# The second half's keys, two blocks of filler matmuls, moved ahead of the first two pool projections in an RWKV-7 mixer

## The chip, the cores and the metric

The kernel runs on one core of a Trainium2 chip. The metric is the time of one execution on the device, in microseconds; runs are compared by their median. Engines are named as in the profile: PE is TensorE (PEld its weight loads), DVE is VectorE, ACT is ScalarE, POOL is GpSimd, SP is SyncE, which issues the loads of weights.

## What is computed

One block of a network on 256 tokens of width 2048, in fp32: a gated feed-forward part, a mixer, and a second gated feed-forward part, each with a norm ahead and behind and a residual. The mixer is what matters here:

```python
def _hybrid_mixer(u, w_in, ...):
    p = u @ w_in
    z_a, z_b, g_a, g_b = jnp.split(p, IN_SPLITS, axis=-1)
    y_a = _rwkv7_branch(z_a, ...) @ w_proj_a
    y_b = _pool_branch(z_b, pool_w, pool_scale) @ w_proj_b
    m = jax.nn.sigmoid(g_a) * y_a + jax.nn.sigmoid(g_b) * y_b
    return m @ w_out
```

`z_a` holds the keys, values and receptances (1024 columns each) of a recurrence over time with 16 heads, and some low-rank inputs. `z_b` goes through four moving averages over time and, per group of 256 columns, a product with `pool_w` (the mix). The two gates `g_a` and `g_b` have 2048 columns each.

## The kernel before

**Products.** Every matrix product is done in three matmuls on rounded parts: a weight tile of 128 x 1024 fp32 is loaded (L118), rounded by ScalarE (wH, L132), and VectorE takes the rest (wL, L133). The loaded tiles have 4 buffers, the parts 5 each. Two generators do the products of the mixer and hand out a cost after each step, so that they can be interleaved:

- `tok_g` (L254): 512 output columns, the tokens in two halves h, so two accumulator banks. A weight tile covers 2 k-steps, which is 12 matmuls (L156 to L158, three for each k and h). At the end an evacuation is called for each half.
- `ch_g` (L285): 256 output columns with the channels on the partitions, in one bank. A weight tile covers 4 k-steps, which is 24 matmuls (L298). At the end one evacuation.

Accumulator banks come from a ring of 4 (tag `mm`), temporaries of 128 x 512 from a ring of 4 (`tmp`, L83). A bank or a temporary is handed out again when its last use is over.

**Pieces of work.** Each is a generator in `mixer` (L537):

- `z_g(hf)` (L595): keys, values and receptances of half `hf` of the heads, in this order, two blocks of `ch_g` for each, with 16 k-steps. The evacuation is `shift` (L522): VectorE scales into a temporary (L527), ScalarE makes a shifted part in a shared buffer `zb` (L531), VectorE combines (L533).
- `gb_g(c)` (L617): a quarter of the second gate, `tok_g` with 16 k-steps. ScalarE evacuates with a sigmoid (L547), into two temporaries that live until the projection of the same quarter.
- `pb_g(c)` (L621): a quarter of the pool's projection, `tok_g` with 8 k-steps, on the scaled mixes `yb`. VectorE multiplies with the gate's temporaries (L625), and GpSimd stores the product to memory (L626). Quarter 0 has its gate from earlier, in a buffer of its own.
- `pool_mix` (L743): the product with `pool_w`; ScalarE scales the result into one part (L751), VectorE makes the other (L752).
- `p_g` (L629): the pool's windows and mixes; behind a `yield None`, the gate of quarter 1 with the last mix put in after 27 of its 32 steps.
- `rwkv` (L759): the recurrence of one half of the heads, a long dependent chain over all engines with few matmuls. It yields how much other work TensorE shall do before the next step.

**Order.** TensorE's order in this part is the order in which the matmuls are written, under a manual schedule. `weave` (L684) takes a step of the recurrence and then as much filler as this asks for. The filler is one sequence, `rest` (L668):

```python
def rest():
    yield from pg          # gate 1, last mix, end of gate 1
    yield from pb_g(0)
    yield from pb_g(1)
    yield from z_g(1)      # keys, values, receptances of half 1
    yield from gb_g(2)
```

and so on. The recurrence of half 0 takes filler up to the gate of quarter 2; that of half 1, which reads `z_g(1)`, follows. VectorE and ScalarE are not under the manual schedule here: their order is set by the framework's scheduler from priorities, which follow the order of emission, with a raised priority for the splits of weights and for the evacuations of `tok_g` and `ch_g`.

In what follows, pn, pV, pk, pA, pB, pb, pM, pX, pU, pSa, pS and pY are the names of the recurrence's results on TensorE in their order.

Of the kernel before, what the change touches and what calls it, by code (L numbers as in the profile page):

```python
# [52 lines left out]
class Block:  # L53
# [483 lines left out]
    def mixer(s, prm, uT, rs, resid, emit, gpost, reload):  # L537
# [54 lines left out]
        yT = [[s.unit((P, 4, S), F32R, n_) for n_ in ("yH", "yL")] for _ in range(2)]  # L592
        z = [{}, {}]

        def z_g(hf):  # L595
            for nme, zc in (("k", 1), ("v", 2), ("r", 0)):
                z[hf][nme] = s.unit((P, 4, S), F32, "z" + nme)
                for b in range(2):
                    c0 = zc * W + hf * 512 + b * 256

                    def ev_z(banks):
                        s.shift(banks[0], P, c0 // P,
                                [z[hf][nme][:, b * 2 + i] for i in range(2)])
                    yield from s.ch_g(w_in, c0, 256, at, NKD, ev_z, 8)
# [12 lines left out]
        def gb_g(c):  # L617
            sg = sgb[c] = [s.tmp("sgb"), s.tmp("sgb")]
            yield from s.tok_g(w_in, GB + c * 512, at, NKD, ev_sig(lambda h: sg[h]))

        def pb_g(c):  # L621
            sg = sgb[c]

            def ev_pb(h, ps):
                nc.vector.tensor_tensor(out=sg[h], in0=ps, in1=sg[h], op=ALU.mult)  # L625
                nc.gpsimd.dma_start(out=msp[c, :, h], in_=sg[h])  # L626
            yield from s.tok_g(prm["w_proj_b"], c * 512, at_b, NKW, ev_pb)
# [18 lines left out]
        def ga_g(c):  # L646
            sg = s.unit((P, 2, 512), F32, "sga")
            sga.append(sg)
            yield from s.tok_g(w_in, GA + c * 512, at, NKD, ev_sig(lambda h: sg[:, h]))
# [16 lines left out]
        pair = s.pair_g(prm["w_proj_a"], (0, 512), at_a, NKW, 4, (ev_pa(0), ev_pa(1)))  # L666

        def rest():  # L668
            yield from pg
            yield from pb_g(0)  # L670
            yield from pb_g(1)
            yield from z_g(1)
            yield from gb_g(2)
            yield from pb_g(2)
            yield from gb_g(3)
            yield from pb_g(3)
            for c in range(4):
                yield from ga_g(c)
            for t in pair:
                if t is None:  # L680
                    return
                yield t
# [8 lines left out]
        with s.tc.manual_schedule(engines={mybir.EngineType.PE}):  # L691
            for _ in s.ch_g(w_in, 3 * W, 288, at, NKD, ev_l, 4):
                pass
            pg = p_g()
            for g in (z_g(0), iter(pg.__next__, None)):
                for _ in g:
                    pass
            fill = rest()
            for hf in range(2):
                weave(chain(hf), fill)  # L700
            for _ in fill:
                pass
# [498 lines left out]
```

## Time and profile before

| | us |
|---|---|
| median of 3 runs | 2101.23 (2100.34 to 2101.69) |
| profiled execution | 2100.07 |
| its span | 2098.4 |
| TensorE busy | 2085.2 |
| VectorE busy | 1254.1 |
| ScalarE busy | 1111.3 |

The span goes from the first to the last instruction. Times in rows are microseconds from its start, unless marked ns; a name such as `sgb<-mm` is what an instruction writes and reads, without buffer numbers. Waits are inferred from semaphores: the engine named is the one that came last. A matmul's duration overlaps that of the next; the distance of their starts is what one costs.

### The profile page before, as it was taken

To read this page: it belongs to the slowest core of one execution; us is meant where nothing else is said; L and a number is where in the kernel's file an instruction comes from. 1 tells how busy PE (TensorE), PEld (TensorE's weight loads), DVE (VectorE), ACT (ScalarE), POOL (GpSimd) and SP (SyncE) were. 2 spreads that over 40 slices of the span, in tenths; PEclk is the share of its full clock that TensorE was granted. 3 is DMA by queue.
4 is the path that set the end of the run, shared out by engine and by line. 5 is a ranking of instruction groups with operands and counts; after the bars stand their busy time and mean duration, and the time that the engine had idled before them with its cause. 6 is when DMAs were issued, how large, how long until landed. Compare 5 with 4: busy or idle time off the path is not lost.

```text
span 2098.4 us, 28820 instructions
## 1 busy us (share of the span) xinstructions
PE 2085.2 (99%) x11089; PEld 1758.4 (84%) x11089; DVE 1254.1 (60%) x1588; ACT 1111.3 (53%) x1600; POOL 74.3 (4%) x161
## 2 busy tenths in 40 slices
PE   9999999999999999999999999999999999999998
PEld 7888888888888899989888788888888888888886
DVE  6555555555444565798688666575555555554444
ACT  6565555655444465464465444466655565554442
POOL 0000000000000010000110110000000000000000
PEclk9999999999999999999999999999999999999999
DMA  7656666577666666656456566666666666676664
GB/s 259 193 176 211 194 192 194 180 217 242 196 194 191 192 199 188 177 174 180 133 154 191 159 247 192 196 217 191 185 204 195 192 188 193 208 245 197 191 193 138
DMA packets 224116, 406.99 MB, mean 194 GB/s; under 512 B 13151, under 2 KB 49129, under 8 KB 223977
## 3 DMA queue, kind: packets, MB, share of 16 engines
q1 hardware_dynamic: 217801, 384.68, 60.0%
q0 software_dynamic: 5888, 19.93, 2.7%
q8 instruction: 87, 1.43, 0.3%
q10 hardware_dynamic: 288, 0.52, 0.1%
q14 instruction: 52, 0.43, 0.1%
HBM read 396.69 MB, written 8.39 MB: 193 GB/s over the span
## 4 chain that ended last, share of the span: by engine, by line
PE 97%; DVE 1%; issue 1%; ACT 0%; DMA 0%; DVEq 0%; POOLq 0%; POOL 0%; SPq 0%; ACTq 0%
PE mm L156 28%; PE mm L158 28%; PE mm L157 28%; PE mc L298 10%; PE tr L326 1%; PE pA L922 0%; DVE wL L133 0%; PE pSa L1030 0%; PE pU L1018 0%; DMA w<-in_ffn_gate_dram 0%; PE pT L1089 0%; PE pM L988 0%; PE pb L951 0%; PE pS L1038 0%; PE pY L1053 0%
## 5 line engine op out<-in xcount | busy, mean ns | idle before, releaser
L133 DVE TENSOR_TENSOR wL<-w,wH 128x1024 fp32r<-128x1024 f32 (+2 forms) x725 | 872.7, 1211 | 741.0 <-ACT wH L132 739.8
L132 ACT CAST wH<-w 128x1024 fp32r<-128x1024 f32 (+2 forms) x725 | 751.0, 1044 | 813.9 <-PE mm L158 665.9
L156 PE MATMUL mm<-wH,xH 128*128 128x512 f32 x2460 | 961.7, 392 | 0.0
L158 PE MATMUL mm<-wH,xL 128*128 128x512 f32 x2460 | 959.1, 390 | 0.7 <-DVE xL L334 0.7
L157 PE MATMUL mm<-wL,xH 128*128 128x512 f32 x2460 | 958.7, 390 | 0.0
L158 PEld LDWEIGHTS mm<-wH,xL 128*128 128x128 f32 x2460 | 461.9, 188 | 97.7 <-DVE xL L334 1.5
L156 PEld LDWEIGHTS mm<-wH,xH 128*128 128x128 f32 x2460 | 462.0, 188 | 96.0 <-ACT xH L332 0.4
L157 PEld LDWEIGHTS mm<-wL,xH 128*128 128x128 f32 x2460 | 462.1, 188 | 94.4 <-DVE wL L133 0.3
L298 PE MATMUL mc<-xH,wH 128*128 128x256 f32 x560 | 159.8, 285 | 0.0
L298 PE MATMUL mc<-xL,wH 128*128 128x256 f32 x560 | 158.7, 283 | 0.0
L298 PE MATMUL mc<-xH,wL 128*128 128x256 f32 x560 | 158.6, 283 | 0.0
L353 ACT COPY x<-T 32x256 f32<-32x256 f32 x352 | 141.8, 403 | 3.9
L298 PEld LDWEIGHTS mc<-xH,wH 128*128 128x128 f32 x560 | 106.1, 189 | 0.9
L298 PEld LDWEIGHTS mc<-xH,wL 128*128 128x128 f32 x560 | 106.1, 189 | 0.3
L298 PEld LDWEIGHTS mc<-xL,wH 128*128 128x128 f32 x560 | 106.1, 189 | 0.1
L372 ACT ACTIVATE sg<-mm,rs 128x512 f32<-128x512 f32 x44 | 29.9, 689 | 22.2 <-PE mm L158 22.2
L373 DVE SCALAR_TENSOR_TENSOR sg<-mm,rs,sg 128x512 f32<-128x512 f32 x44 | 31.5, 750 | 9.2 <-ACT sg L372 9.2
L405 POOL DMA_DIRECT2D gb<-in_ln_ffn_post_dram x4 | 2.4, 592 | 887.8 <-DVE xL L357 854.3
L360 ACT ACTIVATE junk<-mm 128x512 bf16<-128x512 f32 x24 | 14.4, 601 | 36.4 <-PE mm L158 36.4
L378 DVE SCALAR_TENSOR_TENSOR sg<-mm,rs,sg 128x512 f32<-128x512 f32 x44 | 30.9, 743 | 0.0
L343 DVE STREAM_TRANSPOSE T<-sg 128x512 f32<-128x512 f32 x44 | 30.8, 701 | 0.0
L156 PE MATMUL mm<-wH,yb 128*128 128x512 f32 x64 | 26.0, 407 | 1.8 <-ACT sgb L547 1.8
(245 smaller groups left out, 1071.1 us busy)
## 6 DMA issues: line engine op xcount, KB each, us to landing
w<-in_ffn_up_dram SPq DMA_DIRECT2D x176, 512.0 KB
w<-in_ffn_down_dram SPq DMA_DIRECT2D x176, 512.0 KB
w<-in_ffn_gate_dram SPq DMA_DIRECT2D x174, 512.0 KB
w<-in_w_in_dram SPq DMA_DIRECT2D x128, 512.0 KB
w<-in_w_out_dram SPq DMA_DIRECT2D x32, 512.0 KB
w<-in_w_proj_b_dram SPq DMA_DIRECT2D x16, 512.0 KB
w<-in_w_proj_a_dram SPq DMA_DIRECT2D x16, 512.0 KB
hsp<-fg POOLq DMA_DIRECT2D x16, 256.0 KB, 3.4
```

The lines of the kernel that those rows point to most:

```text
L132: s.nc.scalar.copy(vH, v)
L133: s.nc.vector.tensor_tensor(out=vL, in0=v, in1=vH.bitcast(F32), op=ALU.subtract)
L156: nc.tensor.matmul(ps, aH, bH, start=start, stop=False)
L157: nc.tensor.matmul(ps, aH, bL, start=False, stop=False)
L158: nc.tensor.matmul(ps, aL, bH, start=False, stop=stop)
L298: s.nc.tensor.matmul(o, lh, rh, start=one and n == 0, stop=k == KT - 1 and n == 2, skip_group_check=True)
L326: nc.tensor.transpose(ps[:, i], src[:, i * P:(i + 1) * P], s.ident)
L343: s.nc.vector.transpose(out=T1[:, h * 512:h * 512 + 512], in_=src)
L353: nc.scalar.copy(dst[q * 32:q * 32 + 32, :, :, i], src[i * 32:i * 32 + 32, :, :, q])
L372: nc.scalar.activation(out=sg, in_=ps, func=AF.Sigmoid, scale=rs[h])
L373: nc.vector.scalar_tensor_tensor(out=sg, in0=ps, scalar=rs[h], in1=sg, op0=ALU.mult, op1=ALU.mult)
L378: nc.vector.scalar_tensor_tensor(out=sig[h], in0=ps, scalar=rs[h], in1=sig[h], op0=ALU.mult, op1=ALU.mult)
```

## The change

The two blocks of keys of half 1 are taken out of `z_g(1)` and stand behind the pool's last mix (and the rest of gate 1) and ahead of the pool's first projection. Values and receptances stay where they were.

```diff
-        def z_g(hf):
-            for nme, zc in (("k", 1), ("v", 2), ("r", 0)):
+        def z_g(hf, part=0):
+            for nme, zc in ((("k", 1), ("v", 2), ("r", 0)), (("k", 1),),
+                            (("v", 2), ("r", 0)))[part]:
                 z[hf][nme] = s.unit((P, 4, S), F32, "z" + nme)
                 for b in range(2):
                     c0 = zc * W + hf * 512 + b * 256
...
         def rest():
+            z1 = z_g(1, 1), z_g(1, 2)
             yield from pg
+            yield from z1[0]
             yield from pb_g(0)
             yield from pb_g(1)
-            yield from z_g(1)
+            yield from z1[1]
             yield from gb_g(2)
```

## The prediction

> **What bounds the kernel now.** I read the page first, then TensorE's list of waits, the chain of waits around the longest of them, and the timelines of the engines there.
>
> ```profile
> span 2098.4 us, 28820 instructions
> PE 2085.2 (99%) x11089; PEld 1758.4 (84%) x11089; DVE 1254.1 (60%) x1588; ACT 1111.3 (53%) x1600; POOL 74.3 (4%) x161
> PE 97%; DVE 1%; issue 1%; ACT 0%; DMA 0%; DVEq 0%; POOLq 0%; POOL 0%; SPq 0%; ACTq 0%
> ...
> PE mm L156 <- ACT sgb L547: 1.8, 1, 1.8
> PE warm L223 <- POOL ident masks.py:199: 1.7, 1, 1.7
> PE mm L158 <- DVE xL L334: 0.7, 2, 0.5
> PE pSa L1030 <- ACT us L1025: 0.4, 1, 0.4
> PE tr L326 <- DMA x<-in_x_dram: 0.4, 1, 0.4
> ```
>
> The first three rows are the page's: TensorE is busy 2085.2 of 2098.4 us and is 97% of the chain. The other five are its complete list of waits (total, times, longest, in us). All of them together come to 5.0 us in 2098. So a change of order, which takes no instruction away, has little to win: at most these waits, and only one, the first, lies where the change is. The stretch looks like this on TensorE, and on the chain that ends there:
>
> ```profile
> 921.51 0.39 PE L156 MATMUL mm<-wH,yb 128*128 128x512 f32 x1
> 921.74 0.39 PE L157 MATMUL mm<-wL,yb 128*128 128x512 f32 x1
> 921.97 0.39 PE L158 MATMUL mm<-wH,yb 128*128 128x512 f32 x1
> 924.18 0.50 PE L156 MATMUL mm<-wH,yb 128*128 128x512 f32 x1 [1.82 <-ACT sgb L547]
> 924.52 0.40 PE L157 MATMUL mm<-wL,yb 128*128 128x512 f32 x1
> ```
> ```profile
> 921.15 0.48 DVE yb L752
> 921.65 0.47 ACT yb L751
> 922.14 1.28 ACT L547
> 923.44 0.70 ACT sgb L547
> 924.18 0.50 PE mm L156
> ```
>
> At 921.51 the first projection begins (its operand is yb). Three matmuls of its first half run; the first of its second half stands until 924.18. The columns of the second fence are start, duration, what. ScalarE first had the pool's last mix to scale (L751, itself behind VectorE's L752), then an activation table (1.28 us), then the first sigmoid of the gate (0.70 us). That sigmoid empties the bank which the projection's second half wants: of the four accumulator banks the gate took two, the mix the third, the projection's first half the fourth, and its second half comes round to the gate's first. The wait is thus one of the bank ring, one allocation too soon after the gate.
>
> Its price: from 921.97 to 924.18 is 2.21 us where the rows above it are 0.23 apart, so 1.98 lost, and the next step is 0.34 instead of 0.23, 0.11 more. **2.1 us.**
>
> **The change part by part.** TensorE's order is the written one. The two blocks of the second half's keys (z_g, part 1) move from behind the second projection to ahead of the first. Nothing is added or removed: the same loads, splits, matmuls, evacuations and stores.
>
> (a) The wait. A block of keys takes one bank, not two. The first block takes the bank that the first projection's first half has now, which had no wait at 921.51. The second block takes the gate's first bank, a block later.
>
> ```profile
> 963.15 43.91 PE mc L298 x366
> ```
>
> 366 of these matmuls in 43.91 us are 0.12 us each; a block is 16 k-steps of 2 column blocks of 3 matmuls, 96, hence 11.5 us. The gate's bank is asked for at 921.5 + 11.5 = 933.0 and is free at 924.1 by the chain above: 8.9 us to spare. The projections then take the mix's bank, the gate's second, and the two of the keys, each a block or more after its evacuation began. From the values on every bank is the same as before. So the 2.1 us go, and no bank is late next: **-2.1 us.**
>
> (b) The mix. The first projection reads the mix's last part.
>
> ```profile
> 928.09 0.48 DVE L752 SCALAR_TENSOR_TENSOR yb<-mc,cols,yb 128x256 fp32r<-128x256 f32 x1
> ```
>
> It is ready at 928.6, and read from the thirteenth matmul triple of the projection on, at about 931.8 now (924.18 and eleven triples of 0.68). That cover of 3 us becomes more than 20 us. It was no wait, so it is worth 0.
>
> (c) Weight tiles. With the wait gone, TensorE asks for its tiles 2.1 us earlier, while VectorE is nearly full:
>
> ```profile
> 918.00:938.00 20.00, 18.18 (x97) 14.66 (x97) 19.58 (x29) 10.99 (x15) 1.35 (x3) 1.00 0.63 196
> 938.00:958.00 20.00, 20.00 (x159) 17.29 (x156) 16.63 (x24) 14.99 (x32) 2.46 (x5) 1.00 0.70 226
> 958.00:978.00 20.00, 20.00 (x172) 19.59 (x171) 18.86 (x45) 8.31 (x12) 0.00 (x0) 1.00 0.56 153
> ...
> 924.25 1.22 DVE L133 TENSOR_TENSOR wL<-w,wH 128x1024 fp32r<-128x1024 f32 x1
> 929.34 0.39 PE L157 MATMUL mm<-wL,yb 128*128 128x512 f32 x1
> 929.89 1.23 DVE L133 TENSOR_TENSOR wL<-w,wH 128x1024 fp32r<-128x1024 f32 x1
> 934.78 0.39 PE L157 MATMUL mm<-wL,yb 128*128 128x512 f32 x1
> ```
>
> The table's columns after the length are the busy times of TensorE, its weight loads, VectorE, ScalarE and GpSimd, the granted clock, and the DMA share and rate: VectorE is busy 19.58 of 20 us. I counted the splits (L133) back from the steady stretch, where a cast waits for the end of the tile five before it. The split that starts at 924.25 is the third tile of the first projection and is used at 929.34; that of 929.89 is the first tile of the second projection, used at 934.78. They end at 925.47 and 931.12: leads of 3.9 and 3.7 us, or 1.8 and 1.6 us without the 2.1. A key tile lasts 24 x 0.12 = 2.88 us against 12 x 0.23 = 2.76 of a projection, so ahead of the third and the fifth tile, after two and four of them, the leads grow by 0.2 and 0.5, to 2.0 and 2.1 us. The splits hold, if VectorE keeps its order: **0**, with bounds of 0 and the price in rival C.
>
> (d) Evacuations and stores. Within the stretch up to the values they only change places:
>
> ```profile
> L527 DVE TENSOR_TENSOR z<-mc,rsb 128x512 f32<-128x512 f32 x6 | 4.1, 688 | 1.3 <-PE mc L298 1.3
> L531 ACT ACTIVATE zb<-z,cols 128x256 f32<-128x256 f32 x12 | 5.4, 501 | 0.2 <-DVE z L527 0.2
> L533 DVE SCALAR_TENSOR_TENSOR zk<-z,omu,zb 128x256 f32<-128x256 f32 x4 | 1.8, 481 | 0.0
> L625 DVE TENSOR_TENSOR sgb<-mm,sgb 128x512 f32<-128x512 f32 x4 | 2.7, 685 | 0.0
> L626 POOL DMA_DIRECT2D msp<-sgb x4 | 2.2, 559 | 19.0 <-DVE sgb L625 19.0
> ```
>
> A block of keys costs VectorE 0.69 + 2 x 0.48 = 1.65 us and ScalarE 2 x 0.50 = 1.0; a projection costs VectorE 2 x 0.685 = 1.37 and GpSimd two stores. So at about 933 and 946 VectorE has 0.3 us more than now and ScalarE 1.0 us more, and the long chain of small VectorE steps behind it (the recurrence's triangular inverse) has 0.3 us less per block. The recurrence's next step on TensorE is at 936.75:
>
> ```profile
> 931.03 1.38 DVE L898 TENSOR_TENSOR R<-R,R 64x512 f32<-64x512 f32 x2
> ...
> 936.75 1.99 PE pA L922 x32
> ```
>
> Its inputs are complete at 932.4 at the latest. TensorE will be there at 934.7, after the first block of keys (933.0), so 2.3 us lie between. I take 0. The lower bound is 0 as well, since TensorE does not wait there now; the upper is an evacuation of 1.65 us put wholly ahead of the inputs, which is less than the 2.3.
>
> (e) Temporaries. The gate's two tiles now live over the keys' two temporaries; with four buffers that just fits. The values' first evacuation takes the buffer that the second projection's first store frees.
>
> ```profile
> 988.38 0.69 DVE L527 TENSOR_TENSOR z<-mc,rsb 128x512 f32<-128x512 f32 x1 [0.27 <-PE mc L298]
> ...
> DMA to landing us min/median/max: 2.3/4.6/10.2
> ```
>
> The second projection will end where the keys' second block ends now, one block of 11.5 us and the 0.2 of the pipe ahead of that row, 976.7, less 2.1: 974.6. Two multiplications (1.4) and two issues (1.1) make 977.1; the median landing of a store gives 981.7, the worst one of the eight 987.3. The first evacuation of the values is now at 988.38, then at 986.3: 4.6 us to spare at the median, 1.0 us short at the worst, and behind that stand several split tiles. I take 0. [...]
>
> **The sum.** The profiled execution took 2100.07 us, its span 2098.4, so 1.7 lie around it. Less 2.1 it would be 2098.0, with a span of 2096.3. The median of the runs, 2101.23, is 1.16 above the profiled one; less 2.1 it is **2099.1 us**, 0.1% faster. The three runs spread from 2100.34 to 2101.69. About 0.2%, 4.2 us, is what a measurement of this kernel can tell from no change, so this counts as within it.
>
> **The rivals.**
>
> A (forecast), 0.72: the wait goes, nothing takes its place; 2099.1, with the spread of the runs 2098.0 to 2100.2.
>
> B, 0.15: the wait moves. TensorE runs 2.1 us earlier into engines that were not waiting for it, and meets a tile, an input of the recurrence or an evacuation that is late by as much. For it: VectorE at 19.58 of 20 us. Against it: the leads of 2.0 to 2.3 us in (c) and (d), and VectorE at 16.63 in the next stretch. 2101.2; and 2103.2 if a lead of 2 us is lost once more.
>
> C, 0.09, the other side: VectorE's order is not written here but follows from priorities, and a new order of emission can give a new one.
>
> ```profile
> L898 DVE TENSOR_TENSOR R<-R,R 64x512 f32<-64x512 f32 x4 | 2.7, 683 | 0.0
> L903 DVE SCALAR_TENSOR_TENSOR R<-R,R 64x504 f32<-64x504 f32 x4 | 2.7, 673 | 0.0
> ...
> 923.11 1.23 DVE L893 TENSOR_TENSOR R<-R,R 128x1024 f32<-128x1024 f32 x1
> ```
>
> If the recurrence's four L903, four L898 and the L893 between them (1.23 us) come ahead of the splits of the third to fifth tile, with the evacuation of a key block (1.65) and the mix's L752 (0.48), these are 8.8 us against a lead of 2.0: a wait of 6.8 us, 2099.1 + 6.8 = 2105.9. It costs from 2.0 us of delay on, and 0.2% above today's median, 2105.4, is reached at 8.3 us. Against it: the splits have a raised priority, and they do stand between those steps today.
>
> D, 0.04: a gain of more than 4.2 us. All waits of TensorE together are 5.0 us, 1.7 of them before any of this; I see no mechanism.
>
> That the change does not do what it says can hardly be: TensorE's order is fixed by the text.
>
> **How the numbers follow.** Faster by over 0.2%: D, 0.04. Slower by over 0.2%: most of C, 0.08. Within: the rest, 0.88. The range of 8 in 10 takes A and B: from 2097.5 (A, less the spread of the runs once more) to 2103.2 (B with a second lead lost).
>
> **What would show it.** Right: TensorE's list of waits without the row of sgb L547, and no new row above 0.5 us between 915 and 1035; the values begin at about 974.6 instead of 976.7, and everything behind is 2.1 us earlier; the span is 2096.3. Wrong: a wait of a matmul on a DVE wL between 925 and 940 (C), on z or zb between 933 and 950 (B), on a DVE z at 986 that itself waits for a store (e); or a sigmoid of the gate that still ends a wait.

## The result, and the profile after

| | before | after |
|---|---|---|
| median of 22 runs, us | 2101.72 (2099.93 to 2104.48) | 2098.38 (2097.79 to 2101.31) |
| profiled execution, us | 2100.07 | 2101.31 |
| its span, us | 2098.4 | 2099.6 |

The ratio of the runs is 0.9985, with a 95% interval of 0.9979 to 0.9991: 1.9 to 4.4 us faster, in the middle 3.2, or 0.15%. The forecast was 2099.1, that is 2.1 us faster, in a range of 2097.5 to 2103.2.

The profiled execution of the changed kernel is no typical one: it is the slowest of its 22, and its trace has to be read with that in mind. Its span of 2099.6 us is not the forecast 2096.3; the median span of the 22 runs is 2096.7. First its page and TensorE's complete list of waits (total, times, longest):

```profile
span 2099.6 us, 28824 instructions
PE 2087.3 (99%) x11089; PEld 1759.9 (84%) x11089; DVE 1253.8 (60%) x1588; ACT 1112.6 (53%) x1600; POOL 74.3 (4%) x161
...
PE warm L223 <- POOL ident masks.py:199: 1.7, 1, 1.7
PE tr L326 <- DMA x<-in_x_dram: 1.7, 1, 1.7
PE pSa L1033 <- ACT us L1028: 0.4, 1, 0.4
PE mm L158 <- DVE xL L334: 0.2, 1, 0.2
```

The row of `sgb L547`, 1.8 us, is gone, and no row has come in its place in the mixer. What made this execution long is at its very start. The table by stretches shows it (length; busy time of PE, PEld, DVE, ACT, POOL; granted clock; DMA share and rate):

```profile
0.00:10.00 10.00, 6.25 (x26) 4.66 (x26) 2.81 (x9) 4.64 (x12) 2.79 (x32) 0.92 0.76 268
10.00:20.00 10.00, 10.00 (x39) 7.88 (x39) 6.55 (x17) 5.03 (x12) 0.00 (x0) 0.74 1.05 385
20.00:30.00 10.00, 10.00 (x52) 8.23 (x51) 7.04 (x16) 6.57 (x17) 0.00 (x0) 1.00 0.51 188
...
890.00:1035.00 145.00, 145.00 (x1275) 133.58 (x1275) 125.53 (x238) 83.72 (x134) 14.95 (x24) 1.00 0.55 171
```

The matmul that waits for the input x starts at 7.30 us instead of 5.90 (a wait of 1.7 us against 0.4), and the granted clock was 0.92 and 0.74 in the first two stretches. In the changed stretch, the last row, TensorE is busy 145.00 of 145 us. In the profile of before it was 143.18:

```profile
890.00:1035.00 145.00, 143.18 (x1254) 131.02 (x1252) 124.47 (x236) 82.13 (x132) 14.96 (x24) 1.00 0.56 167
```

So that the start does not disturb the comparison, I set the two traces side by side: the start of TensorE's n-th matmul in one against that in the profile of before. Ahead of the change (matmul 4400, at 882 us) the changed kernel is 3.31 us late; behind it (matmul 5200, at 996 us) 1.21 us; at the last matmul 1.25 us. **The changed stretch gained 2.10 us, and nothing was lost or won behind it.** The same comparison is used for every run below.

| run | late at 882 us | late at 996 us | change in the stretch | late at the end |
|---|---|---|---|---|
| after | 3.31 | 1.21 | -2.10 | 1.25 |
| e1, before again | 0.39 | 0.36 | -0.03 | 0.38 |
| e2, first projection by halves | -0.05 | -2.14 | -2.09 | -2.11 |
| e3, keys between the projections | 0.38 | 0.27 | -0.11 | 0.30 |
| e4, gate without sigmoid | 0.90 | -0.56 | -1.46 | -0.52 |
| e5, one block of keys | 1.63 | -0.34 | -1.97 | -0.26 |
| e6, mix last | 0.24 | 3.17 | +2.93 | 3.20 |
| e7, 6.9 us more on VectorE | 0.00 | 9.15 | +9.15 | 9.21 |
| e8, longer gap | 0.37 | -1.74 | -2.11 | -1.07 |
| e9a, before, one more profile | 0.52 | 2.10 | +1.58 | 2.12 |
| e9b, before, one more profile | 0.44 | 0.45 | +0.01 | 0.48 |
| e9c, before, one more profile | 0.83 | 2.42 | +1.59 | 2.43 |
| e10, longer gap in one half | 0.16 | -1.95 | -2.11 | -1.33 |

Two questions were left. Are the 2.10 us the bank-ring wait alone (theory T), or does the keys' new place matter (rival K)? And why do the medians differ by 3.3 us when the traces differ by 2.1?

### The profile page after: what moved, and what is told of

The parts are those of the page before. It is cut to its first block, busy times and chain, and to the rows that moved or that the text cites. A ratio compares the mean times of both kernels' runs of the same rounds, so it can differ in the third digit from the quotient of the medians.

```text
span 2099.6 us, 28824 instructions
## 1 busy us (share of the span) xinstructions
PE 2087.3 (99%) x11089; PEld 1759.9 (84%) x11089; DVE 1253.8 (60%) x1588; ACT 1112.6 (53%) x1600; POOL 74.3 (4%) x161
## 4 chain that ended last, share of the span: by engine, by line
PE 98%; DVE 1%; issue 1%; DMA 0%; ACT 0%; DVEq 0%; POOLq 0%; POOL 0%; SPq 0%; ACTq 0%
PE mm L156 28%; PE mm L158 28%; PE mm L157 28%; PE mc L298 10%; PE tr L326 1%; PE pA L925 0%; DMA w<-in_ffn_gate_dram 0%; PE pSa L1033 0%; PE pU L1021 0%; PE pT L1092 0%; PE pM L991 0%; DVE wL L133 0%; PE pV L862 0%; PE pb L954 0%; PE pn L842 0%
## 5 line engine op out<-in xcount | busy, mean ns | idle before, releaser
L133 DVE TENSOR_TENSOR wL<-w,wH 128x1024 fp32r<-128x1024 f32 (+2 forms) x725 | 872.5, 1211 | 740.2 <-ACT wH L132 738.4
L357 DVE TENSOR_TENSOR xL<-x,xH 128x1024 fp32r<-128x1024 f32 x22 | 26.8, 1218 | 0.0
```

Source lines behind the costliest of these rows:

```text
L133: s.nc.vector.tensor_tensor(out=vL, in0=v, in1=vH.bitcast(F32), op=ALU.subtract)
L357: nc.vector.tensor_tensor(out=dL, in0=x32, in1=dH.bitcast(F32), op=ALU.subtract)
```

## The experiments

**e1: the kernel before, again.**

> The kernel before itself, once more, to see how much of the difference of 3.3 us between the medians lies in the changed stretch. Theory T (the bank-ring wait of 2.1 us is the whole effect of the change; the rest of the 3.3 us is chance at the start of the program, where the profile of the changed kernel lost 3.3 us before 90 us): its profile again has the wait of the first projection on the sigmoid of the gate, 1.8 us, and no other wait above 0.5 us between 890 and 1035; the runs spread by more than 2 us and spans go with the granted clock. Rival V (the wait is longer in other executions, which would make the gain more than 2.1 us): the wait in this profile is clearly longer or shorter than 1.8 us, say by 0.5 us or more.

Median 2100.39 us of 11 runs, ratio to the runs of before 0.9996 (0.9987 to 1.0005). The wait is again 1.8 us, so this profile gives no sign of a wait of another length (rival V); e9 adds three more profiles with the same 1.8 us.

**e2: the same wait taken away in another way**, with the keys left where they were (the kernel before; the diff is abridged, its comments are added, and only the first projection takes the new order).

```diff
-                for h in range(2):
-                    s.mm3(pss[h], ...)       # per k-step: half 0, half 1
+            for (k, wH, wL), h in [(t, h) for h in range(2) for t in ts]:
+                    s.mm3(pss[h], ...)       # per four k-steps: half 0, then half 1
```

> The order of before; only the first projection takes its steps differently: within each four k-steps first all of the first half of the tokens, then all of the second. The gate's bank is then asked for at 921.5 + 4 x 0.68 = 924.2 instead of 922.2, and it is free at 924.1. The keys stay behind the projections. Theory T: the wait falls from 1.8 us to under 0.3, the time by 1.8 to 2.1 us against before, the same as the change. Rival K (it is the keys' place that brings the gain: fewer evacuations beside the recurrence, a longer cover of the mix): the wait is gone but the time stays within 0.7 us of before, or another wait takes its place, such as a matmul on a split tile, for the second tile is asked for 1.4 us earlier.

Median 2098.40 us, ratio 0.9988 (0.9980 to 0.9997). TensorE's timeline, where the second half begins:

```profile
923.96 0.39 PE L158 MATMUL mm<-wH,yb 128*128 128x512 f32 x1
924.19 0.45 PE L156 MATMUL mm<-wH,yb 128*128 128x512 f32 x1
924.47 0.40 PE L157 MATMUL mm<-wL,yb 128*128 128x512 f32 x1
```

Four k-steps of one half are put between the gate's end and the claim on its bank, and the wait is gone: -2.09 us, as much as the change. The keys need not move for it. Theory T holds and rival K falls.

**e3: the keys between the two projections** (against the changed kernel).

```diff
             yield from pg
+            yield from pb_g(0)
             yield from z1[0]
-            yield from pb_g(0)
             yield from pb_g(1)
```

> The keys stand between the first projection and the second, not ahead of both. The first projection again follows the gate directly. Theory T: the wait on the gate's sigmoid is back, 1.8 us, and the time is that of before within 0.7 us. Rival K (an earlier place for the keys, apart from the banks, is what pays): half or more of the gain is kept, 1 us or more below before.

Median 2100.37 us, ratio 1.0000 (0.9991 to 1.0008). Its list of waits:

```profile
PE mm L156 <- ACT sgb L547: 1.8, 1, 1.8
PE warm L223 <- POOL ident masks.py:199: 1.7, 1, 1.7
PE pSa L1033 <- ACT us L1028: 0.4, 1, 0.4
PE tr L326 <- DMA x<-in_x_dram: 0.4, 1, 0.4
```

The keys stand earlier, but behind the first projection, and the wait is back at its full length.

**e4: no table at the gate.** The kernel before, with the sigmoid of the second quarter's gate left out; a scaled copy stands there. The diff is abridged.

```diff
-ev_sig(lambda h: sg[h])
+ev_sig(lambda h: sg[h], AF.Copy if c == 1 else AF.Sigmoid)
```

> The order of before; the gate of the second quarter leaves out its sigmoid (a scaled copy stands in its place), so that ScalarE loads no table there. Theory T, by the chain of before (the mix's scaling, table 1.28 us, sigmoid 0.70 us): the wait falls from 1.82 to about 0.5 us and the time by 1.3 us; the table is loaded at the next gate, near 1050, where nothing waits. Rival Y (the wait is set by the mix on VectorE and ScalarE, and the table is hidden): the wait stays above 1.3 us.

Median 2099.10 us, ratio 0.9992 (0.9983 to 1.0001). ScalarE's timeline and TensorE's one wait there:

```profile
922.55 0.47 ACT L752 ACTIVATE yb<-mc,cols 128x256 fp32r<-128x256 f32 x1 [0.56 <-DVE yb L753]
922.92 1.26 ACT L547 ACTIVATE sgb<-mm,rs 128x512 f32<-128x512 f32 x2
...
923.66 0.50 PE L156 MATMUL mm<-wH,yb 128*128 128x512 f32 x1 [0.41 <-ACT sgb L547]
```

Between the mix's scaling and the evacuation there is no table, and the wait is 0.41 us instead of 1.82. The table accounts for 1.4 us of the wait, the queue behind the mix for the rest. The interval of the medians holds 1, so it is the trace that shows this, with -1.46 us in the stretch.

**e5: only one of the two blocks moved** (against the kernel before, abridged).

```diff
-            yield from z_g(1)                      # behind pb_g(1)
+            yield from z_g(1, (("k", 1, 0),))      # ahead of pb_g(0)
+            ...
+            yield from z_g(1, (("k", 1, 1), ...))  # behind pb_g(1)
```

> Only the first of the two blocks of keys stands ahead of the projections; the second stays behind them. Theory T (the wait is one allocation of the four-bank ring too soon after the gate): one block in one bank is enough, since the first projection then comes round to the gate's banks 11.5 us later; the wait is gone and TensorE gains the whole 2.1 us in this stretch. Rival K (the gain grows with the work that is moved, through the evacuations and the cover of the mix): about half, 1.0 us.

Median 2098.36 us, ratio 0.9989 (0.9980 to 0.9998); -1.97 us in the stretch. One block does it all but 0.13 us; what these come from stays open. The gain does not grow with the work that is moved.

**e6: the mix behind the gate** (against the kernel before).

```diff
-            for t in itertools.islice(gate, 27):
-                yield t
-            yield from s.pool_mix(3, mix, prm["pool_w"], pT)
             yield from gate
+            yield from s.pool_mix(3, mix, prm["pool_w"], pT)
```

> The keys stay behind the projections; the last mix stands behind the whole gate instead of five steps ahead of its end. The gate ends 1.5 us sooner and its sigmoid is no longer queued on ScalarE behind the mix's scaling: table and sigmoid are done at about 922.0, when the projection's second half asks for the bank at 922.2. Theory T: the wait on the sigmoid falls to under 0.4 us. But the mix ends 3.4 us later and its last part, at 928.6 in before, is asked for at 929.7: if it comes 3.4 us later too, a wait of up to 2.3 us on VectorE or ScalarE making yb stands in its place. So between 2.1 us faster and the same as before; the change as made has no such price.

Median 2103.94 us, ratio 1.0014 (1.0005 to 1.0022): slower than before. TensorE's timeline, VectorE's up to the mix's row, and the stretches around it:

```profile
931.57 0.39 PE L157 MATMUL mm<-wL,yb 128*128 128x512 f32 x1
935.11 0.50 PE L158 MATMUL mm<-wH,yb 128*128 128x512 f32 x1 [3.15 <-DVE yb L750]
...
936.82 0.63 PE L158 MATMUL mm<-wH,yb 128*128 128x512 f32 x1
937.25 0.63 PE L156 MATMUL mm<-wH,yb 128*128 128x512 f32 x1
```
```profile
929.49 2.78 DVE L896 TENSOR_TENSOR R<-R,R 64x512 f32<-64x512 f32 x4
932.30 2.36 DVE L133 TENSOR_TENSOR wL<-w,wH 128x1024 fp32r<-128x1024 f32 x2
934.58 0.48 DVE L750 SCALAR_TENSOR_TENSOR yb<-mc,cols,yb 128x256 fp32r<-128x256 f32 x1
```
```profile
930.00:935.00 5.00, 1.96 (x9) 1.30 (x7) 4.93 (x8) 1.04 (x1) 0.00 (x0) 1.00 0.60 189
935.00:940.00 5.00, 4.89 (x15) 3.51 (x17) 3.61 (x5) 1.05 (x1) 1.15 (x2) 0.66 0.97 295
```

The wait on the sigmoid is gone as expected, and the other one stands in its place, with 3.15 us instead of "up to 2.3": the last part of yb is made at 934.58, six microseconds later than in before and not 3.4, for VectorE puts four steps of the recurrence (L896) and two splits ahead of it. But a gain of 2.1 and a wait of 3.2 make +1.1 us, and the trace shows +2.93. Most of the rest is in the last fence: behind the wait the granted clock falls to 0.66 in the mean of five microseconds, and the matmuls start 0.43 us apart (936.82, 937.25) instead of 0.23. That was the first sight of what the medians hid.

**e7: the load of rival C made to happen** (six more operations on VectorE, against the changed kernel).

```diff
+        for _ in range(0 if hf else 6):
+            V.tensor_tensor(out=fl(kk), in0=fl(kk), in1=fl(kk), op=ALU.max)
         V.tensor_tensor(out=fl(a), in0=fl(kk), in1=fl(a), op=ALU.mult)
```

> The changed kernel with six extra VectorE operations of 1.15 us each (6.9 us) in the recurrence of the first half, just ahead of L893; they leave its values as they are. It is the prediction's rival C made to happen: VectorE is given 6.9 us more in the full stretch where the splits lead by 1.9 to 2.1 us. If VectorE's order let the recurrence go ahead of the splits (rival C's mechanism), TensorE waits for split tiles, about 4.8 us in all. If the raised priority of the splits protects them, they keep at least 0.7 us of lead (one operation of 1.2 us put ahead of each) and it is the recurrence that is late: its first products, 4.7 us after their inputs now, wait about 2.2 us. Either way the stretch has room for 2 to 5 us of VectorE work, not for 7.

Median 2109.56 us of 5 runs, ratio 1.0041 (1.0028 to 1.0054). VectorE's timeline and TensorE's wait:

```profile
925.35 1.21 DVE L897 TENSOR_TENSOR R<-R 128x1024 f32<-128x1024 f32 x1
926.48 2.35 DVE L133 TENSOR_TENSOR wL<-w,wH 128x1024 fp32r<-128x1024 f32 x2
928.75 1.21 DVE L897 TENSOR_TENSOR R<-R 128x1024 f32<-128x1024 f32 x1
929.89 1.22 DVE L133 TENSOR_TENSOR wL<-w,wH 128x1024 fp32r<-128x1024 f32 x1
...
942.35 2.82 DVE L903 TENSOR_TENSOR R<-R,R 64x512 f32<-64x512 f32 x4
...
943.18 4.47 PE L927 MATMUL pA<-R,R 64*128 64x128 f32 x32 [8.55 <-DVE R L903]
```

The splits (L133) stand between the extra operations (L897), each as soon as it is ready; no matmul waits for a tile. It is the recurrence that is late, at pA. The stretch has no room for so much more work on VectorE, but rival C's mechanism does not appear: the splits hold, as their raised priority would have it, and the dependent chain pays. It pays more than the 2.2 us expected, 8.55 us for 6.9 us of work, because more splits and a key evacuation now come ahead of its end: seven splits stand between the mix's row at 921.16 and the chain's last step at 942.35, and two in the same part of the changed kernel.

**e8: an attempt at the last wait of the mixer** (against the changed kernel).

```diff
-            yield 1.6
+            yield 2.3 if c == 2 else 1.6
```

> The changed kernel with 0.7 us more filler between two steps of the recurrence (2.3 instead of 1.6 at the third chunk), where TensorE's last wait of the mixer stands, 0.4 us on ScalarE at pSa. If that wait is nothing but too little filler, it goes: 0.4 to 0.5 us faster than the changed kernel in the trace, too little to show in the medians. If the steps behind it are held by the same ScalarE queue, a wait of the same size stands a step later and nothing is gained.

Median 2099.10 us, ratio 0.9992 (0.9983 to 1.0001). Its waits in the mixer, which have taken the place of the 0.4 us at pSa:

```profile
PE pS L1041 <- ACT R L1035: 0.6, 1, 0.6
...
PE pU L1021 <- DVE R L1046: 0.3, 1, 0.3
```

They stand near 1195 and 1202 us, in the other half's recurrence. **e10** puts the longer step into the first half alone:

> The changed kernel with the 0.7 us more filler of e8 only in the recurrence of the first half, where the wait of 0.4 us at pSa stands. In e8 that wait went, but two new ones, 0.6 and 0.3 us, came near 1195 and 1202, in the second half, where there had been none. If they came from the longer step of the second half itself, they are absent here and the trace is 0.4 to 0.5 us shorter than that of the changed kernel behind 1040, 2.5 us shorter than before; if they came from the shift of everything behind the first half, they are here again.

The same two rows are there, 0.6 and 0.3 us. So they come from the shift of what follows; the median is 2098.88 us, ratio 0.9986 (0.9977 to 0.9995). Neither beats the changed kernel, and nothing else here does: e2 and e5 equal it.

**e9: three more profiles of the kernel before.** All runs carry their mean granted clock, but for the 22 of before that stand beside the result. Of 82 runs of before, e1 and e3, which have the wait, 29 have a mean of 0.998 or less (the expectation says 30, a miscount); of 44 runs of after, e2 and e5, which do not, 2. Of 15 later runs of before, taken beside e10, 9 have it.

> The kernel before, a second look of three (e9a to e9c). The medians differ by more than the 2.1 us that the traces show, and the runs of the kernels that have the wait (before, e1, e3) reach mean granted clocks of 0.998 and less in 30 of 82, those without it (after, e2, e5) in 2 of 44. Theory G: in a part of the executions the wait of 1.8 us is followed by a stretch at half the granted clock of TensorE, 3.4 us long as in the profile of e6 behind a wait of 3.2 us, which costs 1.7 us more. Then a look with a mean clock of 0.998 has that stretch within 10 us behind the wait, and its matmuls there start 0.43 instead of 0.23 us apart. Rival H: the lower clock belongs to the start of the program, as in the profile of the changed kernel, and has nothing to do with the wait; then the stretch at half clock lies before 30 us.

> As e9a: the kernel before, the third look. Theory G: where the mean clock is 0.998 or less, half clock for 3.4 us behind the wait at 922 to 924, 1.7 us; where it is 0.999, none. Rival H: half clock, if any, at the start of the program.

> As e9a: the kernel before, the fourth look. Theory G: where the mean clock is 0.998 or less, half clock for 3.4 us behind the wait at 922 to 924, 1.7 us; where it is 0.999, none. Rival H: half clock, if any, at the start of the program.

The three took 2102.16, 2100.53 and 2102.49 us, at mean clocks of 0.998, 0.999 and 0.998. TensorE in the first of them, from its wait on, and then the stretch from 925 to 935 us in the first, the second and the third:

```profile
924.71 0.50 PE L156 MATMUL mm<-wH,yb 128*128 128x512 f32 x1 [1.83 <-ACT sgb L547]
...
926.29 0.63 PE L157 MATMUL mm<-wL,yb 128*128 128x512 f32 x1
926.72 0.63 PE L158 MATMUL mm<-wH,yb 128*128 128x512 f32 x1
...
928.69 0.39 PE L157 MATMUL mm<-wL,yb 128*128 128x512 f32 x1
928.92 0.39 PE L158 MATMUL mm<-wH,yb 128*128 128x512 f32 x1
```
```profile
925.00:935.00 10.00, 10.00 (x38) 8.05 (x38) 9.87 (x14) 4.38 (x7) 0.00 (x0) 0.83 0.48 159
```
```profile
925.00:935.00 10.00, 10.00 (x45) 8.23 (x44) 9.87 (x14) 4.31 (x7) 0.00 (x0) 1.00 0.49 159
```
```profile
925.00:935.00 10.00, 9.98 (x37) 8.06 (x38) 9.87 (x15) 4.36 (x7) 0.00 (x0) 0.83 0.48 157
```

The wait is the same in all three, 1.8 us. In the first and the third it is followed by 3.4 us at half clock (0.83 is the mean over ten microseconds: 0.17 x 10 x 2), with matmuls 0.43 us apart, and in the second it is not. The two cost 1.58 and 1.59 us more in the table above. Theory G is shown for these profiles, and rival H falls for them. Half clock at the start of the program exists as well: the profile of the changed kernel has it (a granted clock of 0.92 and 0.74 in its first two stretches), so a low mean clock alone does not tell which of the two a run had.

## Why the prediction was right, and where it was too small

- **(a) The wait of the bank ring: right.** The term of -2.1 us measured -2.10, and e2, e3, e4 and e5 tie it to the release of the gate's bank and not to the keys' place.
- **(b) The mix: right.** No wait on yb. e6 shows that the cover of about 3 us which it names is real: with yb six microseconds later, the cover is used up and a wait of 3.15 us stands there.
- **(c) Weight tiles: right.** In the changed kernel the splits of the third and fifth key tile and their first uses are these:

```profile
927.57 1.22 DVE L133 TENSOR_TENSOR wL<-w,wH 128x1024 fp32r<-128x1024 f32 x1
930.70 0.28 PE L298 MATMUL mc<-xH,wL 128*128 128x256 f32 x1
933.24 1.23 DVE L133 TENSOR_TENSOR wL<-w,wH 128x1024 fp32r<-128x1024 f32 x1
936.46 0.28 PE L298 MATMUL mc<-xH,wL 128*128 128x256 f32 x1
```

  930.70 - 928.79 = 1.9 us, and 936.46 - 934.47 = 2.0 us, where 2.0 and 2.1 were predicted.
- **(d) Evacuations: right.** pA starts at 937.87, 2.1 us behind its inputs (935.76); predicted were 2.3.
- **(e) Temporaries: right.** The values' first evacuation is at 989.59, 3.31 of it from the late start: 986.28, where 986.3 was predicted, and it waits for no store. The four stores took 0.54 to 0.61 us to issue and landed within 4.1 us at the new place (L627, from 967 to 980 us), beside a VectorE busy 12.62 of 13 us; at the old place (L626) they also took 0.54 to 0.61 us and landed within 5.1. So these profiles show no store that is slower at the new place.
- **The sum: the mechanism right, the size too small.** The step that fell short is the price, "2.1 us", taken for every execution from one profile that happened to keep its clock. In the two profiles with half clock behind the wait, the same wait costs 1.6 us more, and 29 of 82 runs, later 9 of 15, have a mean clock as low as theirs. Among the runs at a mean clock of 0.999 the medians are 2100.34 us (53 runs with the wait) and 2098.36 us (42 without): 2.0 us, which is the trace's 2.1. The rest of the 3.3 us fits this share of half clock in the 22 runs of before, 15 of which took over 2101.5 us, but their clocks are not on record, so this part is argued and not shown.
- **The start of the sum.** That 2099.1 came so near to 2098.38 is in part luck. The sum added to the profiled execution the 1.16 us by which the median of three runs lay above it, and carried them over to the changed kernel. Without them it gives 2098.0, and the measured median is 0.4 above that: most of the 1.16 us was no longer there without the wait.
- **Rivals.** B, C and D did not occur. Even with 6.9 us more for VectorE (e7), it was the recurrence that was late and no split.

## What to carry to other kernels

Before the place of a piece of work is blamed or praised, count the allocations of a small ring between one user and the next: here one block of keys in one bank between the gate and the projection, or four k-steps of one half ahead of the other, was worth the same 2.0 to 2.1 us. Price a stall of TensorE by what stands behind it as well (1.6 us more in e9a and e9c), and take more than one profile where the runs spread: the wait was the same 1.8 us in all five profiles of the kernel before, and the time was not. In e7, where raised priorities protect the feeding of the matmuls, 6.9 us of extra work on VectorE came out at the dependent chain, as a wait of 8.55 us.

## What the runs showed of the hardware

A wait of TensorE of 1.8 us was followed by 3.4 us at half clock in e9a and e9c, and by none in e9b, in e3 and in the first profile of before. In e9a the wait lasts from 922.88 to 924.71, and the clock is 0.50 from 925.09 to 928.50. The clock records of the changed kernel's profile are 3.413 us at full clock (from 5.04), 6.827 at half (from 8.46) and 2078.717 at full; that of before has 2088.957 at full (from 5.14). With a step of 3.4133 us these are 1, 2, 609 and 612 steps, and the half clock of e9a is one. The last record of each, at half clock from 2094.0 and 2094.1 on, runs to the end of the profile. Why the same wait is followed by half clock in one execution and not in another is not shown; 38 of the 97 runs counted above have the lower clock.

How much idle time it takes is not shown either. These are the 3.41 us ahead of the half clock in e9a, as many that hold nearly the whole wait of e3, and the 3.41 us ahead of the half clock at the start of the changed kernel's profile, each with the 3.41 us that follow (length and TensorE's busy time first, the granted clock third from the end):

```profile
921.67:925.09 3.42, 1.59 (x8) 1.00 (x7) 3.38 (x8) 2.88 (x4) 0.53 (x1) 1.00 0.60 210
925.09:928.50 3.41, 3.41 (x10) 2.63 (x9) 3.37 (x6) 1.30 (x4) 0.00 (x0) 0.50 0.33 121
```
```profile
921.12:924.53 3.41, 1.62 (x8) 1.00 (x6) 3.37 (x7) 2.80 (x5) 0.53 (x1) 1.00 0.73 242
924.53:927.94 3.41, 3.37 (x15) 2.80 (x16) 3.37 (x7) 2.68 (x5) 0.00 (x0) 1.00 0.26 64
```
```profile
5.04:8.46 3.42, 1.70 (x10) 1.07 (x10) 0.81 (x2) 1.82 (x6) 0.00 (x0) 1.00 1.03 384
8.46:11.87 3.41, 3.21 (x10) 2.13 (x10) 3.41 (x11) 2.42 (x7) 0.00 (x0) 0.50 1.05 393
```

TensorE is idle for 1.83 us of the first stretch and 1.79 of the second, with the same matmuls, and only the first is followed by half clock. But 1.72 us in the third, at the start, are followed by it too, for 6.83 us. So the idle time alone does not tell the three apart, and what else counts stays open. The longer waits stand beside half clock in the one profile of each: 3.15 us in e6 with 3.4 us of it (0.66 in the mean of five), 8.55 us in e7 with 32 matmuls of pA behind it that take 4.47 us, where they take 2.06 in the changed kernel (the mean clock of that execution is 0.996).
